# The last modulation sections between the sets of chunk inverses, and the second norm's columns inside the first half of the output projection

## The chip, the cores and the metric

One core of a Trainium2 chip runs the whole layer in one launch. The metric is device microseconds of one execution; the kernel before was timed in three runs.

## The reference

One layer of a diffusion backbone over 512 latent tokens (T) and 256 context tokens (TC), width 2048 (D), all in float32. The parts that matter here:

```python
mod = (jax.nn.silu(c) @ w_mod[l] + b_mod[l])[:, None, :]
sh1, sc1, g1, sh2, sc2, g2 = jnp.split(mod, 6, axis=-1)
h = modulate(x, norm_attn_g[l], sh1, sc1)
...
attn = mla_latent_attention(qn, rope_2d(qr, rope_q), keys_nope, keys_rope, values)
...
y, k_sum, _, _ = rwkv_bidirectional(r, k, v, wl, al, s_f, s_b, rw)
rwkv = rwkv_readout(y, r, k_sum, v, gl, gate_up[l], bonus_r_k[l], lnx_g[l], lnx_b[l])
x = x + g1 * (jnp.concatenate([attn, rwkv], axis=-1) @ w_out[l])
x = x + g2 * moe_ffn(modulate(x, norm_ffn_g[l], sh2, sc2), w_grp[l], b_grp[l], w_exp[l], b_exp[l], w1[l], w3[l], w2[l])
return rms_norm(x, final_norm_g)
```

`modulate(x, g, shift, scale)` is `rms_norm(x, g) * (1 + scale) + shift`. `moe_ffn` routes each token to one of 4 groups and to the best 2 of the 8 experts in it; 32 experts with weights of 2048 x 512, 2048 x 512 and 512 x 2048. The modulation's six parts are 2048 wide; sh1 and sc1 are needed at the start, g1 after the output projection, sh2 and sc2 for the router and the experts, g2 after the experts.

## The kernel before

Stages in the order of the trace: the first two parts of the modulation and the first norm; the input projection with its three-pass float32 products (`passes`, L174 to L176); within it, for each of 8 feature blocks f and two directions d, the small Gram matrices of chunks of 64 tokens; the inverses of their triangular blocks; the state chain over 12 chunks with the latent attention beside it; the readouts and the output projection in two halves (attention rows, then recurrent rows); the routing; 16 pairs of experts; the last norm.

**Modulation sections.** `mod_rest` (L510 to L527) makes the other four parts, s = 2, 4, 3, 5 in that order (g1, sc2, sh2, g2), each in four sections of 512 columns: 16 sections. A section is 8 loads of 512 KB issued by POOL (L519), 16 multiplications on ACT (L521), 15 additions on POOL (L523), the bias (L524, L525) and a store to `modr` in DRAM (L526). Its tiles are the five planes of `scr_`. `NM = (6, 0, 0)` lets 6 sections run before the feature blocks; the other 10 are drained after the solves are written down, so beside the chain.

**Chunk inverses.** `solve` (L459 on) inverts 32 x 32 blocks by substitution, 31 steps of a product and a sum (L479, L480), between loads of `r_ab` (L466) and stores to `r_tt` and `r_tn`; `SOLVES` has three sets. POOL makes sets 0 and 1 for both directions (one pass each) after the feature blocks 3 and 5, and set 2 for direction 0; DVE makes set 2 for direction 1. On POOL the tiles are again the planes of `scr_`; a pass ends with a copy (L483).

**Chain and filler.** `run_chain` has 12 steps for each direction. A step loads its factors on SP's queue (QXr, Lr, QYr, AYr and the inverses TNr, TFr), and multiplies: X (L813), Yp (L830), Zp (L842), Sp (L851), Yq (L865); pp and p2 (L796, L803) prepare the inverse of the next step. Yp and Yq exist from the fifth step on. Between these the generator `filler` gives pieces of attention (`mla`: sp are the scores, ptt the transposed probabilities, po the values' product) and then of the first half of the output projection (`attn_out`, `out_loop(0, ...)`: 32 units of 12 products, po_s, po_a, po_o and po_w by PSUM bank). A scheduler decides from this text, when the kernel is built, what each engine's queue holds in which order; tiles with the same buffer keep the order of the text. The last eight units use the same three PSUM banks ("rw") as the chain and the readouts.

**Readouts and second half.** `readout` (L868 to L892) treats 64 tokens: two products with `bones` (rom L882, rov L886), a square root on ACT, a reciprocal on DVE (L888) and four more DVE operations. Then `cat` is split from Y and `out_loop(1, ...)` makes the second half (po_r), with `route_chunk` after every 512 columns.

**The second norm's columns.** `cols` holds 1 + sc2 times the norm's gain, and sh2, as columns. They are made from the partial sums in `modr` by products with a column of ones (L1271, pcl, 4 products of one column for each of 8 loads `mr` on SP's queue, one buffer), written down after the output projection's first half and before its second.

Of the kernel before, what the change touches and what calls it, by code (L numbers as in the profile page):

```python
# [9 lines left out]
F32 = mybir.dt.float32  # L10
# [4 lines left out]
OP = mybir.AluOpType  # L15
# [4 lines left out]
D = 2048  # L20
# [4 lines left out]
C = 64  # L25
NT = T + TC
NP0 = 2
NM = (6, 0, 0)
NFILL = 12
NEARLY = 8  # L30
XU = 8
# [49 lines left out]
def layer(ctx, tc, tab, x, c, ctx_in, c_ctx, w_mod, b_mod, norm_attn_g, norm_ffn_g, w_in, shift_mu,  # L81
# [5 lines left out]
    ve, sc, gp, te, sy = nc.vector, nc.scalar, nc.gpsimd, nc.tensor, nc.sync  # L87
# [6 lines left out]
    modr = dram.tile([128, 4 * D], F32, name="modr")  # L94
# [30 lines left out]
    ones = cp.tile([128, 128], F32, name="ones")  # L125
# [29 lines left out]
    def bank(name, shape, tag, bufs):  # L155
        return ps[tag].tile(shape, F32, name=name, tag=tag, bufs=bufs)
# [129 lines left out]
    with tc.tile_pool(name="p0", bufs=1, side="right") as p0:  # L286
# [52 lines left out]
        n = 0  # L339
# [44 lines left out]
        for src, n, dst, g, width, a, b in ((cqT, 4, r_cq, qg, 512.0, 0, 512),):  # L384
# [5 lines left out]
            v, r, u = nv[:, 0:m], nr[:, 0:m], nu[:, 0:m]  # L390
# [35 lines left out]
        for src, n, dst, g, width, a, b in ((ckvT, 2, r_ckv, kvg, 256.0, 0, 512),  # L426
# [6 lines left out]
            v, r, u = nv[:, 0:m], nr[:, 0:m], nu[:, 0:m]  # L433
# [681 lines left out]
    def mod_row(pool, name, s, tags, e1=ve.tensor_copy):  # L1115
        t_ = pool.tile([128, D], F32, name=name)
        sc.dma_start(t_, modr[:, (s - 2) * D:(s - 1) * D])
        for n in range(4):
            pr_ = bank("prr", [128, 512], *tags[n % len(tags)])
            te.matmul(pr_, ones, t_[:, 512 * n:512 * n + 512], start=True, stop=True)  # L1120
            (sc.copy if n % 2 else e1)(t_[:, 512 * n:512 * n + 512], pr_)
        return t_
# [3 lines left out]
    late = {}  # L1126
# [4 lines left out]
    def out_loop(hf, cat, tags, after=None):  # L1131
        wo, xm = late["wo"], late["xm"]
        for n in range(4):
            ns = slice(512 * n, 512 * n + 512)
            po = tags(n)
            for k in range(8):
                raw = wo.tile([128, 512], F32, name="wor", bufs=4)
                w_ = [wo.tile([128, 512], F32R, name=f"wo{i}", bufs=3) for i in range(2)]
                sc.dma_start(raw, wo_v[:, 8 * hf + k, ns])
                split(w_[0], w_[1], raw, ve)  # L1140
                for i in range(4):
                    passes(po[i], [c_[:, k, 128 * i:128 * i + 128] for c_ in cat], w_, k == 0, k == 7)
                late["w"] = w_[1]
                yield
            for i in range(4):
                t_ = wo.tile([128, 512], F32, name="wt_", bufs=2)
                ve.tensor_mul(t_, po[i], late["g1r"][:, ns])
                ve.tensor_add(xm[:, i, ns], xm[:, i, ns], t_)
            if after:
                after(n)  # L1150
# [7 lines left out]
    def attn_out():  # L1158
        xmp = late["xmp"] = ctx.enter_context(tc.tile_pool(name="xmp", bufs=1))
        wo = late["wo"] = wos.enter_context(tc.tile_pool(name="wo", bufs=1))  # L1160
        cat = cat_tiles()
        for k in range(8):
            t_ = wo.tile([128, T], F32, name="wt_", bufs=2)
            sc.dma_start(t_, r_at[k])
            split(cat[0][:, k], cat[1][:, k], t_)
        late["ro"] = ros.enter_context(tc.tile_pool(name="ro", bufs=1))
        xm = late["xm"] = xmp.tile([128, 4, D], F32, name="xm")
        units = out_loop(0, cat, tags_a)
        xv = x[0].rearrange("(i p) d -> p i d", p=128)
        for u in range(32):  # L1170
            next(units)
            yield
            if u % 8 == (XG if u < 8 else XH):
                ns = slice(512 * (u // 8), 512 * (u // 8) + 512)
                ve.tensor_copy(xm[:, :, ns.start:ns.start + 1], late["w"][:, None, 0:1].to_broadcast([128, 4, 1]))
                for i in range(0, 4, XI):
                    sy.dma_start(xm[:, i:i + XI, ns], xv[:, i:i + XI, ns])
            if u == XG:
                late["g1r"] = mod_row(wo, "g1r", 2, [("a", 1)])
        yield from units  # L1180

    def filler():
# [66 lines left out]
    def t(name, shape, dt=F32, bufs=1):  # L1249
        return rp.tile(shape, dt, name=name, bufs=bufs)  # L1250
# [6 lines left out]
    cst = t("cst", [128, 36])  # L1257
    sy.dma_start(cst[:, 0:4], bass.AP(tensor=b_grp.tensor, offset=b_grp.offset, ap=[[0, 128], [1, 4]]))
    sy.dma_start(cst[:, 4:36], bass.AP(tensor=b_exp.tensor, offset=b_exp.offset, ap=[[0, 128], [1, 32]]))
    gc = t("gc", [128, 4, 4])  # L1260
    sy.dma_start(gc, norm_ffn_g[0].rearrange("(n p j) -> p n j", p=128, j=4))
    cols = xmp.tile([128, 2, 4, 4], F32, name="cols")
    scc, shc = cols[:, 0], cols[:, 1]
    pcl = bank("pcl", [128, 2, 4, 4], "tr", 2)
    for s in range(2):
        for n in range(4):
            mr = t("mr", [128, 512])
            sy.dma_start(mr, modr[:, (2 - s) * D + 512 * n:(2 - s) * D + 512 * n + 512])
            mv = mr.rearrange("t (p j) -> t j p", j=4)
            for j in range(4):  # L1270
                te.matmul(pcl[:, s, n, j:j + 1], mv[:, j], ones[:, 0:1], start=True, stop=True)  # L1271
    fetch(NY + NA)
    ve.tensor_copy(cols, pcl)
    ve.scalar_tensor_tensor(scc, scc, 1.0, gc, op0=OP.add, op1=OP.mult)
    wrs = t("wrs", [128, 4, 4, 36])
    ve.tensor_mul(wrs, wr, scc[:, :, :, None].to_broadcast([128, 4, 4, 36]))
    ve.tensor_mul(wr, wr, shc[:, :, :, None].to_broadcast([128, 4, 4, 36]))
# [412 lines left out]
```

## Time and profile before

| | us |
|---|---|
| median of 3 runs (lowest to highest) | 2669.04 (2664.29 to 2672.88) |
| the profiled execution | 2665.13 |
| its span | 2663.3 |
| PE busy | 2411.0 (91%) |
| DVE busy | 1406.2 (53%) |
| ACT busy | 914.1 (34%) |
| POOL busy | 737.8 (28%) |

The share of an engine over the whole span says little here, since the stages have different limits; the rows below are by stretches of the span. Times in the rows are microseconds from the span's start. The granted clock is that of PE, 1.00 being 2.4 GHz.

### The profile page before, as it was taken

The numbers are of one execution on the slowest core, as the hardware profiler recorded it, in microseconds if no ns is written. First come the engines' busy times: TensorE is split into PE (matmuls) and PEld (weight loads), VectorE is DVE, ScalarE is ACT, GpSimd is POOL, SyncE is SP. The second block draws the span as 40 slices with busy tenths as digits, with TensorE's granted clock in tenths as the row PEclk, the third lists the DMA queues.
The fourth block names the chain that finished last, engine by engine and source line by source line (L and its number), as shares of the span: only waits on it lengthen the run. The fifth ranks groups of instructions, "written<-read, shape, count | busy, mean of one in ns | idle before, by whom it ended". The sixth has DMA issues, their size and how long they took to land. (4 is left out here: it accounts for less than half of the span.)

```text
span 2663.3 us, 39444 instructions
## 1 busy us (share of the span) xinstructions
PE 2411.0 (91%) x15238; PEld 1535.9 (58%) x15238; DVE 1406.2 (53%) x2094; ACT 914.1 (34%) x1659; POOL 737.8 (28%) x830
## 2 busy tenths in 40 slices
PE   4999899998997789998968997999999999999995
PEld 2567678887876667777736785434333334334332
DVE  3345687666778767666458545243333334334324
ACT  4245564332333256554534332311111112112202
POOL 1046654016677544554535300000000000000000
PEclk9999999998997789999989997999999999999998
DMA  8965577665667768788687532999999999999995
GB/s 307 345 189 173 190 195 185 135 141 131 150 136 183 175 180 224 223 243 237 189 271 216 193 131 106 411 421 421 421 421 420 418 421 420 420 416 417 420 421 212
DMA packets 521998, 727.50 MB, mean 273 GB/s; under 512 B 320792, under 2 KB 399536, under 8 KB 471376
## 3 DMA queue, kind: packets, MB, share of 16 engines
q1 hardware_dynamic: 410512, 578.97, 62.0%
q0 software_dynamic: 24208, 83.50, 9.5%
q10 hardware_dynamic: 87088, 62.48, 8.1%
q8 instruction: 121, 1.98, 0.3%
q14 instruction: 69, 0.57, 0.1%
HBM read 659.69 MB, written 73.54 MB: 275 GB/s over the span
## 5 line engine op out<-in xcount | busy, mean ns | idle before, releaser
L523 POOL TENSOR_TENSOR scr<-scr 128x512 f32<-128x512 f32 x240 | 327.7, 1365 | 350.5 <-ACT scr L521 331.2
L174 PE MATMUL acc<-hT,w 128*128 128x512 f32 (+1 forms) x752 | 268.7, 357 | 13.0 <-DVE km L276 9.9
L175 PE MATMUL acc<-hT,w 128*128 128x512 f32 (+1 forms) x752 | 268.9, 358 | 0.0
L176 PE MATMUL acc<-hT,w 128*128 128x512 f32 (+1 forms) x752 | 268.3, 357 | 0.0
L1455 POOL DMA_INDIRECT xg<-r_x,ix x16 | 19.1, 1196 | 831.1 <-DVE sp L1440 627.3
L521 ACT ACTIVATE scr<-scr,scl 128x512 f32<-128x512 f32 x256 | 170.4, 715 | 174.8 <-DMA scr<-in_w_mod_dram 140.6
L1600 PE MATMUL py<-ew,gT 128*64 128x512 f32 x680 | 213.8, 607 | 7.9 <-ACT gT L1580 6.7
L1500 DVE TENSOR_TENSOR xm<-xm,pox 128x512 f32<-128x512 f32 x256 | 161.4, 682 | 62.1 <-PE pox L1499 61.5
L171 DVE TENSOR_TENSOR w<-wraw,w 128x512 fp32r<-128x512 f32 (+1 forms) x132 | 110.8, 845 | 140.8 <-ACT w L170 139.7
L1575 DVE SCALAR_TENSOR_TENSOR scr<-ph,ga,scr 128x512 f32<-128x512 f32 x16 | 12.0, 751 | 310.4 <-PE ph L1556 310.4
L1490 DVE TENSOR_TENSOR yt<-py,g2r 128x512 f32<-128x512 f32 x64 | 42.7, 687 | 242.1 <-PE py L1600 228.7
L174 PEld LDWEIGHTS acc<-hT,w 128*128 128x128 f32 (+1 forms) x752 | 144.5, 192 | 36.2 <-issue 15.4
L176 PEld LDWEIGHTS acc<-hT,w 128*128 128x128 f32 (+1 forms) x752 | 143.9, 191 | 22.4 <-issue 1.4
L175 PEld LDWEIGHTS acc<-hT,w 128*128 128x128 f32 (+1 forms) x752 | 144.5, 192 | 20.4 <-issue 1.0
L170 ACT CAST w<-wraw 128x512 fp32r<-128x512 f32 (+1 forms) x132 | 80.5, 613 | 217.7 <-PE acc L175 125.3
L1600 PEld LDWEIGHTS py<-ew,gT 128*64 128x64 f32 x680 | 73.5, 138 | 125.7 <-issue 109.2
L519 POOL DMA_DIRECT2D scr<-in_w_mod_dram x128 | 92.9, 726 | 173.7 <-DVE scr L358 140.7
L170 ACT CAST yr<-yt 128x512 fp32r<-128x512 f32 x64 | 39.3, 619 | 294.3 <-DVE yt L1490 293.0
L479 POOL TENSOR_TENSOR scr<-scr 128x31 f32<-128x31 f32 (+15 forms) x155 | 108.5, 700 | 27.7 <-DMA scr<-r_ab 16.0
L480 POOL TENSOR_TENSOR scr<-scr 128x31 f32<-128x31 f32 (+15 forms) x155 | 108.1, 697 | 12.1
L1498 PE MATMUL pox<-yr,ohT 128*128 128x512 f32 x256 | 105.6, 428 | 4.1 <-ACT yr L170 3.8
L1572 ACT ACTIVATE scr<-ph 128x512 f32<-128x512 f32 x16 | 9.6, 597 | 260.2 <-PE ph L1556 260.2
(702 smaller groups left out, 5381.9 us busy)
## 6 DMA issues: line engine op xcount, KB each, us to landing
ew<-in_w_dram SPq DMA_DIRECT2D x279, 1024.0 KB, 19.8
Y<-in_w_dram SPq DMA_DIRECT2D x70, 1024.0 KB, 19.5
scr<-in_w_mod_dram POOLq DMA_DIRECT2D x128, 512.0 KB, 5.3
scr<-in_w_dram SPq DMA_DIRECT2D x34, 1024.0 KB, 19.8
ld<-in_w_mod_dram SPq DMA_DIRECT2D x32, 1024.0 KB, 7.3
wraw<-in_w_in_dram ACTq DMA_DIRECT2D x104, 256.0 KB, 3.5
wor<-in_w_out_dram ACTq DMA_DIRECT2D x64, 256.0 KB, 3.3
QXr<-r_qx SPq DMA_DIRECT2D x24, 512.0 KB, 6.0
```

The source lines that it names most:

```text
L170: sc.copy(hi, src)
L171: (lo_eng or ve).tensor_sub(lo, src, hi)
L174: te.matmul(out, lhs[0], rhs[0], start=first, stop=False)
L175: te.matmul(out, lhs[0], rhs[1], start=False, stop=False)
L176: te.matmul(out, lhs[1], rhs[0], start=False, stop=last)
L479: e.tensor_mul(z, xs.to_broadcast([128, n, m]), ms.to_broadcast([128, n, m]))
L480: e.tensor_add(xo, xo, z)
L521: sc.mul(wt[:, k] if kt + k else macc, wt[:, k], scl[:, kt + k:kt + k + 1])
L523: gp.tensor_add(macc, macc, wt[:, k])
L1498: te.matmul(po, ohT[0:np_, 128 * i:128 * i + 128], yr[0], start=True, stop=False)
L1500: ve.tensor_add(xm[:, i, ns], xm[:, i, ns], po)
L1600: te.matmul(pys[n][64 * e:64 * e + 64], gT[:, j, 64 * e:64 * e + 64], ws[e][:, n], start=(j == 0), stop=(j == 3))
```

## The change

`NM` becomes `(6, 3, 3)`: three modulation sections are written down after set 0 of the inverses, three after set 1; the last four are drained after set 2, as ten were before. The columns are made by a new function inside `attn_out`, after units 10 and 18 of the first half, with loads on ACT's queue and a PSUM bank that the first half uses; their old place before the second half is gone.

```diff
-NM = (6, 0, 0)
+NM = (6, 3, 3)
...
         units = out_loop(0, cat, tags_a)
+        cols = late["cols"] = xmp.tile([128, 2, 4, 4], F32, name="cols")
+
+        def mod_cols(s):
+            if s == 0:
+                late["gc"] = wo.tile([128, 4, 4], F32, name="gc")
+                sc.dma_start(late["gc"], norm_ffn_g[0].rearrange("(n p j) -> p n j", p=128, j=4))
+            pcl = bank("pcl", [128, 4, 4], "a", 1)
+            for n in range(4):
+                mr = wo.tile([128, 512], F32, name="wt_", bufs=2)
+                sc.dma_start(mr, modr[:, (2 - s) * D + 512 * n:(2 - s) * D + 512 * n + 512])
+                mv = mr.rearrange("t (p j) -> t j p", j=4)
+                for j in range(4):
+                    te.matmul(pcl[:, n, j:j + 1], mv[:, j], ones[:, 0:1], start=True, stop=True)
+            ve.tensor_copy(cols[:, s], pcl)
+            if s == 0:
+                ve.scalar_tensor_tensor(cols[:, 0], cols[:, 0], 1.0, late["gc"], op0=OP.add, op1=OP.mult)
+
...
             if u == XG:
                 late["g1r"] = mod_row(wo, "g1r", 2, [("a", 1)])
+            if u in (10, 18):
+                mod_cols(0 if u == 10 else 1)
...
-    gc = t("gc", [128, 4, 4])
-    sy.dma_start(gc, norm_ffn_g[0].rearrange("(n p j) -> p n j", p=128, j=4))
-    cols = xmp.tile([128, 2, 4, 4], F32, name="cols")
+    cols = late["cols"]
     scc, shc = cols[:, 0], cols[:, 1]
-    pcl = bank("pcl", [128, 2, 4, 4], "tr", 2)
-    for s in range(2):
-        for n in range(4):
-            mr = t("mr", [128, 512])
-            sy.dma_start(mr, modr[:, (2 - s) * D + 512 * n:(2 - s) * D + 512 * n + 512])
-            mv = mr.rearrange("t (p j) -> t j p", j=4)
-            for j in range(4):
-                te.matmul(pcl[:, s, n, j:j + 1], mv[:, j], ones[:, 0:1], start=True, stop=True)
     fetch(NY + NA)
-    ve.tensor_copy(cols, pcl)
-    ve.scalar_tensor_tensor(scc, scc, 1.0, gc, op0=OP.add, op1=OP.mult)
```

The built order shows where POOL's work went. POOL's queue at the end of the first set of inverses, before (scr are the planes of `scr_`):

```order
L480 TENSOR_TENSOR scr<-scr 128x31
L483 COPY scr<-scr 128x1024
L467 MEMSET scr 128x1024
L468 MEMSET scr 128x32
L466 DMA scr<-r_ab 32x1024
L466 DMA scr<-r_ab 16x1024 x4
```

And the same place now, up to the second set, with the repeating middle left out:

```order
L480 TENSOR_TENSOR scr<-scr 128x31
L483 COPY scr<-scr 128x1024
L519 DMA scr<-in_w_mod_dram 128x2x512 x2
L523 TENSOR_TENSOR scr<-scr 128x512 x2
...
L524 DMA scr<-in_b_mod_dram 1x16x32
L523 TENSOR_TENSOR scr<-scr 128x512 x2
L467 MEMSET scr 128x1024
L468 MEMSET scr 128x32
L525 TENSOR_TENSOR scr<-scr 1x512
L526 DMA modr<-scr 128x512
L913 MEMSET SV_8201 64x8x64 x2
L913 MEMSET SV_8217 64x8x64 x2
```

Three sections stand between the first set's last copy and the second set's loads; three more stand in the same way between the second and the third set. The memsets of the chain's first tiles (L913) moved ahead of the second set.

PE's queue at the chain's first products, before (p is the p2 of the text, po and pqn belong to the attention):

```order
L1079 MATMUL ptt<-k_ident,p 128x128 x8
L803 MATMUL p_8320<-TFr,pps 32x32 x16
L813 MATMUL X<-SV_8201,QXr 64x64 x11
L174 MATMUL po<-pT_7582,vv_7060 128x256
L813 MATMUL X<-SV_8201,QXr 64x64 x5
L813 MATMUL X<-SV_8217,QXr 64x64 x4
```

And now (po_s is a product of the first half of the output projection, L1181 is the new place of pcl):

```order
L174 MATMUL po_s<-wo_13550,cat_12984 128x512
L803 MATMUL p_8320<-TFr,pps 32x32 x16
L813 MATMUL X<-SV_8201,QXr 64x64 x16
L813 MATMUL X<-SV_8217,QXr 64x64 x16
L1181 MATMUL pcl<-ones,wt__13481 128x1 x4
L1181 MATMUL pcl<-ones,wt__13487 128x1 x2
L842 MATMUL Zp<-Xs,TFr 64x64 x32
```

All of the attention and 14 of the 32 units of the first half moved ahead of the first X; 10 more units stand among the first four steps.

PE's queue in a late step of the chain (the ninth), before (sp is a product of the scores):

```order
L813 MATMUL X<-SV_10237,QXr 64x64 x16
L813 MATMUL X<-SV_10251,QXr 64x64 x16
L830 MATMUL Yp<-QYr,SV_10237 64x64 x7
L174 MATMUL sp<-kn_10423,qn_10326 128x512
L175 MATMUL sp<-kn_10424,qn_10326 128x512
L176 MATMUL sp<-kn_10423,qn_10327 128x512
```

And a late step now, in full:

```order
L813 MATMUL X<-SV_11145,QXr 64x64 x16
L813 MATMUL X<-SV_11159,QXr 64x64 x16
L830 MATMUL Yp<-QYr,SV_11145 64x64 x16
L842 MATMUL Zp<-Xs,TFr 64x64 x16
L830 MATMUL Yp<-QYr,SV_11159 64x64 x16
L842 MATMUL Zp<-Xs,TFr 64x64 x16
L796 MATMUL pp<-TNr,AXr 32x32 x16
L851 MATMUL Sp<-SV_11145,Lr 64x64 x16
L796 MATMUL pp<-TNr,AXr 32x32 x16
L851 MATMUL Sp<-SV_11159,Lr 64x64 x16
L803 MATMUL p_11871<-TFr,pps 32x32 x16
L865 MATMUL Yq<-AYr,SV_11145 64x64 x16
```

Only the chain's own products are left in the last eight steps. Behind the last step stand the eight readouts, and behind these the last eight units of the first half.

## Rows read from the trace of the kernel before

**Rows 1.** Busy time in stretches; x counts instructions, then PE's clock, DMA share, GB/s.

```profile
core 0: us, PE busy (x) PEld busy (x) DVE busy (x) ACT busy (x) POOL busy (x), PEclk, DMA share, GB/s
200.00:250.00 50.00, 47.10 (x246) 38.11 (x245) 22.77 (x27) 25.82 (x42) 32.19 (x29) 0.99 0.58 171
400.00:450.00 50.00, 49.27 (x268) 41.34 (x268) 39.76 (x44) 21.95 (x35) 29.59 (x27) 0.93 0.81 193
690.00:850.00 160.00, 145.10 (x779) 117.74 (x778) 129.54 (x151) 61.47 (x90) 115.29 (x158) 0.91 0.72 160
960.00:1340.00 380.00, 356.46 (x5739) 285.93 (x5738) 236.94 (x390) 210.84 (x410) 199.67 (x190) 0.96 0.77 218
1340.00:1498.00 158.00, 119.55 (x422) 84.11 (x422) 111.84 (x125) 64.62 (x106) 76.92 (x70) 0.89 0.75 237
1664.00:2646.00 982.00, 942.60 (x3924) 383.64 (x3920) 336.59 (x556) 198.62 (x435) 17.84 (x15) 1.00 0.99 408
```

**Rows 2.** POOL in order of time: start, duration, then idle time and its releaser.

```profile
706.35 1.97 POOL L483 COPY scr<-scr 128x1024 f32<-128x1024 f32 x1
...
736.22 0.49 POOL L466 DMA_DIRECT2D scr<-r_ab  x1 [19.87 <-DMA r_ax<-AX]
...
854.76 2.59 POOL L483 COPY scr<-scr 128x1024 f32<-128x1024 f32 x1
...
872.92 0.97 POOL L466 DMA_DIRECT2D scr<-r_ab  x2 [10.12 <-DMA r_ax<-AX]
...
933.28 2.02 POOL L483 COPY scr<-scr 128x1024 f32<-128x1024 f32 x1
```

**Rows 3.** The store that ends a modulation section, on POOL in order of time.

```profile
194.49 0.58 POOL L526 DMA_DIRECT2D modr<-scr  x1
...
238.59 0.57 POOL L526 DMA_DIRECT2D modr<-scr  x1
...
388.95 0.57 POOL L526 DMA_DIRECT2D modr<-scr  x1 [0.30 <-POOL scr L525]
...
444.29 0.59 POOL L526 DMA_DIRECT2D modr<-scr  x1 [0.20 <-POOL scr L468]
...
991.99 0.57 POOL L526 DMA_DIRECT2D modr<-scr  x1
...
1254.03 0.57 POOL L526 DMA_DIRECT2D modr<-scr  x1
```

**Rows 4.** PE in order of time: chain products and the first readout.

```profile
971.61 0.91 PE L813 MATMUL X<-SV,QXr 128*64 128x64 f32 x22
...
1109.28 0.69 PE L796 MATMUL pp<-TNr,AXr 32*32 32x32 f32 x32
...
1121.03 1.15 PE L813 MATMUL X<-SV,QXr 128*64 128x64 f32 x32
...
1153.54 3.52 PE L813 MATMUL X<-SV,QXr 128*64 128x64 f32 x64
...
1338.23 1.13 PE L882 MATMUL rom<-Y,k_bones 128*128 128x512 f32 x2
```

**Rows 5.** DMA from 1120 to 1250 us: SP's queue, and one kind of load.

```profile
q1 hardware_dynamic: 27874, 19.24, 54.9%
...
QXr<-r_qx SPq DMA_DIRECT2D x8, 512.0 KB, 6.6
```

**Rows 6.** DVE in order of time: reciprocals of two readouts, one between them.

```profile
1376.02 3.35 DVE L888 RECIPROCAL sq<-sq 128x512 f32<-128x512 f32 x1 [0.72 <-ACT sq L887]
...
1391.60 3.35 DVE L888 RECIPROCAL sq<-sq 128x512 f32<-128x512 f32 x1 [1.27 <-ACT sq L887]
```

**Rows 7.** PE in order of time: last eight units, then the columns' products.

```profile
1470.99 0.61 PE L174 MATMUL po_w<-wo,cat 128*128 128x512 f32 x2
...
1495.09 0.39 PE L176 MATMUL po_a<-wo,cat 128*128 128x512 f32 x1
1499.75 2.00 PE L1271 MATMUL pcl<-ones,mr 128*128 128x1 f32 x8 [4.28 <-issue]
...
1548.29 1.80 PE L1271 MATMUL pcl<-ones,mr 128*128 128x1 f32 x8
```

**Rows 8.** One group of the page's fifth part: busy, mean ns, idle before, releaser.

```profile
L521 ACT ACTIVATE scr<-scr,scl 128x512 f32<-128x512 f32 x256 | 170.4, 715 | 174.8 <-DMA scr<-in_w_mod_dram 140.6
```

## The prediction

> **What bounds the kernel now.** I read the stretches first. From 1664 us to the end the sixteen DMA engines are busy 0.99 of the time and move 408 GB/s [rows 1]: the expert weights stream in, and whatever the engines do there is hidden behind them. So a microsecond won or lost before the experts begin moves the end by one, and the question is only when the second half of the output projection can start, since it and the routing (1498 to 1664 us) follow in one piece. Before that lie three stretches. Up to about 935 us POOL makes the chunk inverses in three sets, and the last set is what the state chain waits for: its copy ends at 935.30 us (933.28 + 2.02) and the chain's first product X starts at 971.61 us [rows 2, 4]. From 960 to 1340 us the twelve steps of the chain run with the attention in their gaps, and PE is busy 356.46 of 380 us (0.94) at a granted clock of 0.96: this stretch is bound by PE's work, not by the chain's waits [rows 1]. From 1340 to 1498 us the eight readouts run beside the first half of the output projection, PE busy 119.55 of 158 us. The last matmul of that half ends at 1495.5 us [rows 7], and I use this as the mark: what the mark moves, the end moves.
>
> **Three sections before the second set.** POOL ends set 0 at 708.32 us [rows 2]. In the new order three modulation sections stand next on POOL, and all of them use the five scratch planes that the solves use, so nothing can pass them. A section took 44.1 us between two stores at 194 and 239 us, and 55.3 us between those at 389 and 444 us [rows 3]. DVE was busy 22.77 of 50 us beside the first and 39.76 of 50 beside the second; in 690 to 850 us it is busy 129.54 of 160, the same 0.8 as beside the slow one [rows 1]. So I take 54 us, with 44 and 55.3 as the ends. 708 + 3 (the stores of the set must land) + 162 = 873 us. What is queued behind: ACT does 16 multiplies a section at 715 ns, and over 16 sections it waited 140.6 us for their loads, 8.8 us a section [rows 8]. Three sections put 34 us of work and 26 us of waits among the weight casts of the input projection, where ACT is busy 61 of 160 us; I cost this at nothing, because what comes next waits for POOL anyway. If that cover were gone it would be at most the 26 us of waits.
>
> **Second set, three more sections, third set.** The second set ran from its last load at 736.22 to 857.35 us, 121 us, in two passes [rows 2]; with 3 us of loads it goes from 873 to 997 us. The 19.87 us that it waited for a store before is gone, since the store is long done. Three more sections, now beside attention: between the stores at 991.99 and 1254.03 us five sections took 52.4 us each [rows 3]; 157 + 3 gives 1157 us. The third set took 62.4 us from its last load, 65 us with loads: 1222 us. From the end of the set to the first X it took 36.3 us before; PE's queue is emptier there now, I take 30: **the chain starts at 1252 us instead of 971.6**. That is the price of the move, 280 us on POOL in front of the chain. The small memsets of the chain's first tiles were moved ahead of it and cost nothing.
>
> **What hides it.** PE doesn't stand still: the order puts the three remaining pairs of attention heads and 14 of the 32 units of the output projection ahead of the first X, and 10 more units between the first four steps. But that was the work that stood in the chain's gaps, and from the fifth step on the chain now runs alone. Its own PE work: 32 records of an X group take 1.15 us, of a pp group 0.69 us [rows 4]. A late step has 64 records each of X, Yp, Zp, Sp and Yq (5 times 2.3) and of pp and p2 (2 times 1.4): 14.3 us; a step before the fifth has no Yp and Yq, 9.7 us. Its loads: the SP queue kept the DMA engines busy 54.9% of 130 us in which 8 QXr loads were issued, that is four steps, 17.8 us a step [rows 5]. So a late step alone costs at least 17.8 us by its loads, and at most what it cost with attention between, (1338.23 - 971.61) / 12 = 30.6 us. I take 20 us, near the loads, because each load can only be issued when the product before it has freed its buffer. An early step I take at 18 us: 9.7 us, 7 us for two and a half units, and a little wait. The chain: 4 x 18 + 8 x 20 = 232 us, end at 1484 us, against 1338 before.
>
> **After the chain.** Before, readouts and projection shared the 158 us. Now the eight readouts stand alone: two gaps between reciprocals took 15.58 us together, 7.8 us each [rows 6], so 58 us to the last variance. Then the last eight units of the first half, which need the banks that chain and readouts held: 24.5 us (1470.99 to 1495.48) [rows 7]. 1484 + 58 + 24.5 = 1566 us for the mark, against 1495.5: **71 us later**.
>
> **The columns.** 32 one-column products leave the second half of the projection. They stood there as eight groups of 1.80 us [rows 7] in a stretch where PE is busy without a break: 14.4 us saved, bounds 0 (if DVE or the weight casts take over as bound) and 18.7 (with the 4.28 us of idle time before the first group, which I think is the change of PSUM pools and stays). The same products in the first half go into idle time of PE between chain steps: nothing, at most 14.4 us. Their eight loads move from the SP queue to ACT's, one load of the norm's gain with them: SP issues loads of 0.3 us less each in a stretch where it waits, nothing.
>
> **Sum.** +71 - 14.4 = +57 us on the profiled execution's 2665.1 us (span 2663.3): 2722 us. The median of the runs is 3.9 us above that execution, which is inside what I can tell.
>
> **A rule against the change.** From 1340 to 1498 us, where PE had gaps and was busy 119.55 of 158 us, the granted clock was 0.89 against 0.96 before it [rows 1], and at the lower of the two levels, 1.2 GHz, 64 X records took 3.52 us where they take 2.30 at 2.4 GHz [rows 4]. The Trainium skill, "TensorE: Matmul & The Clock Gate", section on how HAM oscillation bites in real kernels, says that a matmul loop with idle gaps between its bursts falls back to the lower clock at every gap. By that rule the chain alone would run at the lower clock from its fifth step to the end of the readouts; by the row it would keep about 0.89, and I go by the row. The rule's time is rival two.
>
> **Rivals.** One, the other side: PE stays the bound and the work is only put in another order. PE had 356 + 119 = 476 us of work from 960 us to the mark; at the 0.94 of the middle stretch that ends 507 us after 960, at 1467 us: -28 - 14.4, 2622 us. For it speaks that attention and half the projection fill the wait for POOL; against it the lonely last eight steps and the readouts, where nothing is left to fill PE with. It wins from the point where the chain ends before 1427 us (1495.5 + 14.4 - 24.5 - 58), 57 us earlier than I think: sections at 44 us give 55 of these. Two, the chain at the lower clock: PE's 14.3 us become 14.3 x 3.52 / 2.30 = 21.9, a step 24 us instead of 20 late and 22 instead of 18 early (+48 us), and the last eight units nearly twice as long (+22): 2792 us. Three, the loads: the last four sections of the modulation now run from 1222 us beside the chain, 16.8 MB, 77 us at the 218 GB/s of the chain's stretch [rows 1]. Half of that not hidden is +38 us: 2760 us. That the change doesn't reorder POOL is excluded, the order shows it.
>
> **How the numbers follow.** Forecast 0.62 (2722 us), rival one 0.08, two 0.15, three 0.15. The unknown terms of the forecast are six sections (down to -55, up to +7), twelve steps (8 late ones at 17.8 give -18, at 24 +32), the wait from set to first X, and the columns (-4, +14). The range 2672 to 2790 leaves out rival one, the upper half of rival two and a thin tail. A measurement here can tell about 0.3%, 8 us. Faster by more than that: 0.08, rival one and nothing of the forecast. Within it: 0.07, the forecast's low end. Slower: 0.85.
>
> **What would show it.** In the changed kernel: the copies that end the second and third set near 997 and 1222 us (873 if sections move for free, then I am wrong at the first step); first X near 1252 us, with PE's wait there on POOL's or the inverse's load, not on attention; X to X about 20 us in the last eight steps; the first readout near 1484 us, reciprocals 7.8 us apart; PE busy clearly below 0.8 from 1320 to 1540 us and its clock below 0.9; no one-column products in the second half, and that half about 14 us shorter. I am wrong if the first X comes before 1200 us or the chain alone takes less than 190 us.

## The result, and the profile after

The changed kernel takes 2821.66 us (median; 2816.96 to 2825.04) where the kernel before took 2670.96 us on the same chip: ratio 1.0574, 95% interval [1.0543, 1.0604]. It is slower, as forecast, but by 151 us instead of 57, and outside the range of the prediction. The profiled execution took 2825.04 us, its span 2823.2 us, 159.9 us more than before.

The mark of the prediction, the last matmul of the first half of the output projection, comes at 1669.3 us (1495.5 before, 1566 forecast). From the mark to the first `ph` product of the experts it is 146.3 us (1815.63 - 1669.3) where it was 160.3, and from there to the end 1007.6 us where it was 1007.5. So the whole loss lies ahead of the mark, +174 us, and 14 us come back behind it. The mark and the first `ph`, on PE in order of time:

```profile
1668.90 0.39 PE L176 MATMUL po_a<-wo,cat 128*128 128x512 f32 x1
...
1815.63 1.98 PE L1563 MATMUL ph<-Y,xT__15067 128*64 128x512 f32 x4 [0.20 <-ACT xT__15067 L1490]
```

The stretches that answer to those from 960 us on in [rows 1] (PE busy, PEld, DVE, ACT and POOL busy, then PE's granted clock, DMA share, GB/s):

```profile
960.00:1230.00 270.00, 219.13 (x990) 161.03 (x988) 140.31 (x241) 111.06 (x213) 171.99 (x231) 0.83 0.28 82
1230.00:1293.00 63.00, 54.00 (x322) 42.06 (x323) 27.49 (x39) 21.20 (x38) 33.37 (x45) 0.86 0.81 242
1293.00:1400.00 107.00, 93.51 (x1461) 80.01 (x1456) 60.87 (x93) 45.41 (x86) 54.45 (x50) 0.80 0.90 254
1400.00:1500.00 100.00, 59.50 (x1498) 55.57 (x1495) 34.75 (x54) 37.69 (x71) 48.58 (x46) 0.71 0.87 240
1500.00:1585.00 85.00, 71.84 (x1909) 67.00 (x1904) 43.44 (x72) 20.33 (x47) 0.00 (x0) 0.79 0.83 214
1585.00:1672.00 87.00, 49.55 (x119) 26.39 (x119) 63.97 (x66) 19.09 (x30) 1.09 (x5) 0.74 0.45 128
sum 712.00, PE 547.52 PEld 432.05 DVE 370.83 ACT 254.78 POOL 309.48; mean PE 91.25 PEld 72.01 DVE 61.80 ACT 42.46 POOL 51.58
```

From 960 us to just behind the mark, before had 538 us with PE busy 476.0 and idle 62.0 [rows 1]; after has 712 us with PE busy 547.5 and idle 164.5. The 174 us are thus 102 us of new idle time and 72 us of longer busy time. The work on PE is nearly the same, with some 15 us of the columns in it; it ran at a granted clock of 0.71 to 0.86, where [rows 1] has 0.96 and 0.89. The first line is attention without the chain (PE busy 0.81, DMA share 0.28: of PE's 51 idle us 22.1 are waits for its own softmax, p on ACT); lines three to five are the chain without attention (DMA share 0.83 to 0.90), in the first of them with ten units of the projection.

POOL's queue in order of time, the ends of sections (L526) and of passes of the inverses (L483), answering to [rows 2, 3]:

```profile
715.21 1.97 POOL L483 COPY scr<-scr 128x1024 f32<-128x1024 f32 x1
788.93 0.57 POOL L526 DMA_DIRECT2D modr<-scr  x1
846.71 0.57 POOL L526 DMA_DIRECT2D modr<-scr  x1
931.70 0.59 POOL L526 DMA_DIRECT2D modr<-scr  x1 [0.30 <-POOL scr L525]
...
1052.33 1.96 POOL L483 COPY scr<-scr 128x1024 f32<-128x1024 f32 x1
...
1203.63 0.59 POOL L526 DMA_DIRECT2D modr<-scr  x1 [0.20 <-POOL scr L468]
1253.24 2.11 POOL L483 COPY scr<-scr 128x1024 f32<-128x1024 f32 x1
```

The first three sections took 214 us (717.2 to 931.7), the second set 123, the next three sections 149, the third set 52. The longest wait of that first stretch (waiter, what it waited for, total, times, longest):

```profile
POOL scr L523 <- ACT scr L521: 105.3, 14, 16.2
```

POOL waited for ACT's multiplications half of the time. ACT's own queue in the third section shows why (ACTq are loads that ACT's queue issues):

```profile
874.05 1.33 ACT L521 ACTIVATE scr<-scr,scl 128x512 f32<-128x512 f32 x2
...
883.40 0.48 ACTq L1004 DMA_DIRECT2D wraw<-in_w_ukv_dram  x1
883.92 0.62 ACT L170 CAST cqn<-p 128x512 fp32r<-128x512 f32 x1 [8.55 <-DVE AY L651]
887.87 1.50 ACT L669 COPY L<-pq 128x1024 f32<-128x1024 f32 x2 [3.33 <-PE pq L668]
889.25 0.63 ACT L170 CAST cqn<-p 128x512 fp32r<-128x512 f32 x1
891.97 0.58 ACT L1015 COPY p<-pqr 128x512 f32<-128x512 f32 x1 [2.08 <-PE pqr L176]
892.65 0.58 ACT L679 COPY rs<-pb 128x512 f32<-128x512 f32 x1
895.70 0.72 ACT L684 ACTIVATE rs<-rs,pc 128x512 f32<-128x512 f32 x1 [2.46 <-DVE rs L683]
896.33 1.32 ACT L521 ACTIVATE scr<-scr,scl 128x512 f32<-128x512 f32 x2
```

Between two pairs of multiplications of 0.7 us lie 21 us, in which ACT did 5 us of other work and waited for DVE and PE 16 us (8.55, 3.33, 2.08 and 2.46). A queue keeps its order, so POOL got its next block only then.

PE where the chain starts, then some of its twelve steps and the first readout, answering to [rows 4]:

```profile
1275.30 0.24 PE L796 MATMUL pp<-TNr,AXr 32*32 32x32 f32 x2 [0.23 <-DMA TNr<-r_tn]
...
1292.99 2.08 PE L813 MATMUL X<-SV,QXr 128*64 128x64 f32 x64
...
1400.07 2.19 PE L813 MATMUL X<-SV,QXr 128*64 128x64 f32 x36
1428.46 1.76 PE L813 MATMUL X<-SV,QXr 128*64 128x64 f32 x33
1465.57 1.65 PE L813 MATMUL X<-SV,QXr 128*64 128x64 f32 x26
1495.11 2.08 PE L813 MATMUL X<-SV,QXr 128*64 128x64 f32 x64
1515.42 1.79 PE L813 MATMUL X<-SV,QXr 128*64 128x64 f32 x54
...
1584.75 2.07 PE L882 MATMUL rom<-Y,k_bones 128*128 128x512 f32 x2
```

The first X comes at 1293.0 us (971.6 before), the chain takes 291.8 us (366.6 before, with attention in it). Its first four steps take 107 us, the next three 28, 37 and 30, the last five 20.3 and less. PE reached the chain's first products at 1275 us and waited only 0.23 us for the inverses: POOL and PE's own queue were ready at the same time.

### The profile page after: what moved, and what is told of

Its sections match the earlier page's. It is cut to its first block, busy times and chain, and to the rows that moved or that the text cites. A ratio compares the mean times of both kernels' runs of the same rounds, so it can differ in the third digit from the quotient of the medians.

```text
span 2823.2 us, 39528 instructions
## 1 busy us (share of the span) xinstructions
PE 2477.2 (88%) x15238; PEld 1592.5 (56%) x15238; DVE 1413.7 (50%) x2095; ACT 913.8 (32%) x1659; POOL 720.4 (26%) x830
## 5 line engine op out<-in xcount | busy, mean ns | idle before, releaser
L523 POOL TENSOR_TENSOR scr<-scr 128x512 f32<-128x512 f32 x240 | 333.5, 1389 | 364.0 <-ACT scr L521 347.4
L174 PE MATMUL acc<-hT,w 128*128 128x512 f32 (+1 forms) x752 | 273.7, 364 | 12.6 <-DVE km L276 9.7
L175 PE MATMUL acc<-hT,w 128*128 128x512 f32 (+1 forms) x752 | 273.5, 364 | 0.0
L176 PE MATMUL acc<-hT,w 128*128 128x512 f32 (+1 forms) x752 | 272.2, 362 | 0.1
L174 PEld LDWEIGHTS acc<-hT,w 128*128 128x128 f32 (+1 forms) x752 | 147.7, 196 | 37.2 <-issue 15.1
L176 PEld LDWEIGHTS acc<-hT,w 128*128 128x128 f32 (+1 forms) x752 | 146.9, 195 | 23.8 <-issue 2.1
L175 PEld LDWEIGHTS acc<-hT,w 128*128 128x128 f32 (+1 forms) x752 | 147.6, 196 | 21.1 <-issue 1.2
L480 POOL TENSOR_TENSOR scr<-scr 128x31 f32<-128x31 f32 (+15 forms) x155 | 101.0, 651 | 12.2
L479 POOL TENSOR_TENSOR scr<-scr 128x31 f32<-128x31 f32 (+15 forms) x155 | 94.2, 608 | 28.6 <-DMA scr<-r_ab 16.9
L171 DVE TENSOR_TENSOR wo<-wor,wo 128x512 fp32r<-128x512 f32 x64 | 50.0, 787 | 99.8 <-ACT wo L170 93.2
```

The lines of the kernel that those rows point to most:

```text
L171: (lo_eng or ve).tensor_sub(lo, src, hi)
L174: te.matmul(out, lhs[0], rhs[0], start=first, stop=False)
L175: te.matmul(out, lhs[0], rhs[1], start=False, stop=False)
L176: te.matmul(out, lhs[1], rhs[0], start=False, stop=last)
L479: e.tensor_mul(z, xs.to_broadcast([128, n, m]), ms.to_broadcast([128, n, m]))
L480: e.tensor_add(xo, xo, z)
```

## The experiments

Theory one: the six sections delay the third set on POOL, and what is lost is the overlap of chain and attention. Theory two: the sections cost in their new places, by ACT's queue and their loads. Theory three: the chain alone is slowed by the last four sections' loads beside it. All times below are medians, "more" is against the kernel before in the same comparison.

**The two parts apart.** First the columns alone:

```diff
-NM = (6, 3, 3)
+NM = (6, 0, 0)
```

> The columns inside the first half, but all ten sections again behind the solves (NM back to 6, 0, 0). If the price is the delay of the third set by the six sections and the columns are a gain of their own, the eight groups of 1.80 us leave the second half and cost nothing in the gaps of the chain: 14 us less than before, about 2656 us. If the columns' products cost in the chain's busy stretch what they saved later, it is the time before, 2668 to 2673 us. If the columns have a part in the changed kernel's long early steps, it is slower than before, up to 2690 us.

Measured: 2667.84 us, ratio 1.0011 [0.9986, 1.0037]. No gain. In the profiled execution, the longest of the twelve (2676.93 us), the mark comes 25 us later than before (1520.8) and the second half is 13 us shorter. The products stand here behind the last readout, eight groups on PE from 1444 to 1489 us.

In that stretch PE is not idle. From the last readout's products to the mark (before, then columns alone):

```profile
1429.00:1498.00 69.00, 61.68 (x256) 48.43 (x254) 49.78 (x59) 30.75 (x51) 43.74 (x37) 0.98 0.68 214
```

```profile
1427.00:1523.00 96.00, 86.49 (x338) 71.44 (x336) 61.28 (x69) 32.94 (x55) 51.11 (x44) 0.89 0.63 204
```

The eight groups went from one busy stretch of PE to another. Then the sections alone, `NM = (6, 3, 3)` in the kernel before:

> The kernel before with NM = (6, 3, 3), the columns in their old place. If the sections carry the whole price, the mark (last matmul of the first half) is 174 us later as in the changed kernel and the second half keeps its 14 us: 2836 to 2846 us. If the columns between the first chain steps made part of the price, it is below the changed kernel's 2822 us, with the first four steps shorter than their 107 us.

Measured: 2819.16 us, 1.0572 [1.0529, 1.0615], below the expected 2836 and the same as the changed kernel's 1.0574. The sections carry the whole price, and the columns are worth nothing beside them that could be told (the two intervals are 8 and 11 us to each side): without them the chain's first four steps take 91.5 us (1271.9 to 1363.4) instead of 107.1, with them the second half is 14 us shorter. A trace of one execution has its limits here: the first set ends 10.8 us earlier in this profile than in the changed kernel's, though both programs are the same up to there.

**What slows a section between the sets.** The six moved sections multiply on POOL instead of ACT (here and in the next such cut the condition that picks these six is left out):

```diff
-sc.mul(wt[:, k] if kt + k else macc, wt[:, k], scl[:, kt + k:kt + k + 1])
+gp.tensor_scalar_mul(wt[:, k], wt[:, k], scl[:, kt + k:kt + k + 1])
 gp.tensor_add(macc, macc, wt[:, k])
```

> The changed kernel, but the six moved sections are multiplied on POOL (a multiplication in place and an addition, both 128 x 512) and no longer on ACT. If ACT's queue set the pace of the sections (72, 58 and 85 us for the first three, where POOL waited 105 us for ACT), a section now takes two POOL operations of about 1.2 us for each of 16 blocks, 35 to 42 us, the second set ends 60 to 90 us earlier, the first X comes 80 to 130 us before 1293 us and the time falls by 60 to 110 us, to 2710 to 2760 us. If the loads set the pace, the sections stay at 50 us or more and the time is above 2790 us. If only the chain beside the last four sections is at fault, the time falls by less than 20 us.

Measured: 2879.93 us, 1.0805 [1.0755, 1.0854], slower than the changed kernel; the sections took 78, 76 and 112 us. It doesn't tell the theories apart, since two new costs came with it. From 715 to 930 us, POOL's groups (busy, mean ns, idle before):

```profile
L527 POOL TENSOR_SCALAR scr<-scr,scl 128x512 f32<-128x512 f32 x36 | 68.4, 1906 | 23.7 <-DMA scr<-in_w_mod_dram 23.7
L528 POOL TENSOR_TENSOR scr<-scr 128x512 f32<-128x512 f32 x33 | 50.2, 1522 | 1.3
...
L920 POOL MEMSET SV<- 64x512 f32 x4 | 2.1, 518 | 42.0 <-DVE Y L479 41.8
```

A multiplication and an addition take 3.4 us on POOL, not 2.4, and the memsets of the chain's first tiles, which the new order put into the third section, waited 41.8 us for memory that DVE's solve still used. So the next kernel leaves the multiplications of the six sections out, and puts those memsets on DVE:

```diff
-sc.mul(wt[:, k] if kt + k else macc, wt[:, k], scl[:, kt + k:kt + k + 1])
 gp.tensor_add(macc, macc, wt[:, k])
...
-gp.memset(st_[0, d]["SV"][half_[hh], :, hh, :], 0.0)
+ve.memset(st_[0, d]["SV"][half_[hh], :, hh, :], 0.0)
```

> The changed kernel, but the six moved sections do no multiplication on ACT (POOL adds the loaded blocks as they are; the scaling is left out), and the memsets of the chain's first tiles stand on DVE. If POOL waits in a section for ACT's queue (105 of the 215 us of the first three), a section is left with 16 operations of 1.4 us and 8 issues of 0.7 us, 30 to 40 us: the third set ends at about 1110 us for 1255, and the time falls to 2690 to 2740 us. If the loads set the pace, sections stay at 50 us or more and the time is above 2790 us.

Measured: 2796.10 us, 1.0488 [1.0453, 1.0522], and neither expectation holds whole: the time is above 2790 us, but not because the sections kept their length. The first three sections took 150 us instead of 214, the next three 117 instead of 149: 64 us of the first three went with the multiplications, and the loads and POOL's own work set a floor of 38 to 60 us a section. But the third set ended only 40 us earlier, at 1215.6, because the second set took 182 us instead of 123: its first pass's stores on SP's queue came late. POOL, in order of time:

```profile
928.27 1.98 POOL L483 COPY scr<-scr 128x1024 f32<-128x1024 f32 x1
986.58 0.95 POOL L467 MEMSET scr<- 128x1024 f32 x1 [56.33 <-DMA r_tt<-scr]
...
1004.66 1.92 POOL L466 DMA_DIRECT2D scr<-r_ab  x4 [15.52 <-DMA r_tn<-scr]
```

SP's queue keeps its order, and in front of these stores it waited for DVE's own solve and for an attention output's store:

```profile
SPq L486 <- DMA r_at<-ao: 16.8, 1, 16.8
SPq L485 <- DVE Y L480: 15.2, 1, 15.2
```

And of the 40 us only 12 arrived at the first X (1280.7), which PE's queue now reached 65 us after the set: attention and 14 units of the projection stand ahead of it. So the sections on POOL are not the only thing that sets the start; the order on PE that was built with them is a second one, as late.

**Loads beside the chain.** The last four sections do one of their eight loads:

```diff
-for kt in range(0, KT, 2):
+for kt in range(0, KT if s < 5 else 2, 2):
```

> The changed kernel, but the last four sections (g2) load and add only the first of their eight blocks; seven eighths of that sum are left out. In the changed kernel these four run from 1256 to 1485 us, beside the chain, and the steps beside them take 28, 37 and 30 us where the steps after them take 20, 20, 19 and 17. If their 16.8 MB slow the chain, the late steps all take 17 to 21 us, the chain is 40 to 70 us shorter than its 292 us and the time falls to 2750 to 2785 us. If the chain's pace is its own (its loads, its waits, the clock), the steps stay and the time is above 2810 us.

Measured: 2775.81 us, 1.0415 [1.0367, 1.0464], 46 us less than the changed kernel. The first X is where it was (1290.4), the first four steps take 92 us for 107, the last eight 156 for 185. From 1400 to 1500 us, the DMA queues (packets, MB, share; q1 is the chain's loads, q0 the sections') and the busy times, first of the changed kernel, then of this one:

```profile
q1 hardware_dynamic: 24017, 15.49, 59.9%
q0 software_dynamic: 2208, 8.26, 25.9%
```

```profile
1400.00:1500.00 100.00, 80.96 (x2184) 75.30 (x2184) 51.23 (x87) 25.93 (x60) 0.00 (x0) 0.81 0.86 222
...
q1 hardware_dynamic: 32500, 21.87, 84.2%
```

The DMA engines are equally busy, 0.87 and 0.86; what the sections took, 26%, the chain takes when they are gone, and PE is busy 81 us instead of 59.5. The last four sections thus cost the chain 44 us. But the edit takes their multiplications on ACT away together with their loads, and the waits of the changed kernel say how they cost. First three waits from 1293 to 1585 us, then ACT and PE (last line) around one of them:

```profile
ACT scr L521 <- DMA scr<-in_w_mod_dram: 82.3, 23, 11.1
PE Yp L830 <- ACT Xs L815: 17.4, 2, 9.0
PE Sp L851 <- DMA Lr<-r_l: 0.6, 1, 0.6
```

```profile
1439.52 1.33 ACT L521 ACTIVATE scr<-scr,scl 128x512 f32<-128x512 f32 x2 [11.12 <-DMA scr<-in_w_mod_dram]
1440.87 0.58 ACT L815 COPY Xs<-X 128x512 f32<-128x512 f32 x1
1441.51 1.97 PE L830 MATMUL Yp<-QYr,SV 128*64 128x64 f32 x32 [8.40 <-ACT Xs L815]
```

The chain's copy of X stands on ACT behind two multiplications of a section, these wait for the section's load, and PE waits for the copy. Each of PE's seven waits for ACT between 1400 and 1500 us, 32 us together, ends with a copy that stands right behind such a multiplication. From 1293 to 1585 us PE waited 40 us for ACT's copies and 1.2 us for the chain's own loads. Without seven eighths of the sections' work it is 4 and 13 us in the 249 us from 1290 on. So theory three holds for 44 us in its size, but the way there is mainly ACT's queue, of which theory two spoke, and not a chain whose own loads come late. A kernel with the loads beside the chain and without the multiplications was not tried.

**Delay alone.** The kernel before with all sections where they were, but the zeros in the chain's first tiles made from the last attention output:

```diff
-gp.memset(st_[0, d]["SV"][half_[hh], :, hh, :], 0.0)
+ve.tensor_scalar_mul(st_[0, d]["SV"][half_[hh], :, hh, :],
+                     late["aol"][half_[hh]].rearrange("p (f v) -> p f v", f=NF), 0.0)
...
+    while "ro" not in late:
+        next(fill)
```

The last two lines write all of the attention down ahead of the chain.

> The kernel before with all its sections in their old places (NM = 6, 0, 0, columns late), but the zeros of the chain's first tiles are made as 0 times the last attention output, so that the chain can't start before attention is done. No set of inverses is later. If the price of the change is that attention and chain no longer run in each other's gaps, attention alone ends at about 1210 us, the chain starts 20 us later, and the time is 2780 to 2830 us, as the changed kernel's. If the price comes from the sections in their new places (ACT's queue, the loads, POOL), it is far below: under 2730 us.

Measured: 2757.71 us, 1.0328 [1.0291, 1.0364], between the two expectations. No set is late here (the third ends at 942.0 us), and the first X comes at 1216.1 us. The stretches up to X, and the chain:

```profile
942.00:1190.00 248.00, 209.38 (x1050) 153.50 (x1050) 128.49 (x234) 131.07 (x248) 146.03 (x141) 0.84 0.42 127
...
1216.00:1482.00 266.00, 207.21 (x3812) 173.52 (x3814) 146.23 (x215) 110.04 (x208) 115.75 (x107) 0.85 0.91 263
```

Attention alone keeps PE busy 0.84 at a clock of 0.84, much as in the changed kernel's first line. So 91 of the 151 us come without any section in a new place, from a chain that starts 245 us later; the other 60, by difference, come with a start 77 us later still. Four sections run beside the chain here too (the last store at 1464.8 us), so what they cost it is in the 91.

**Is there a free part?** Three sections in one place only, then one, and four more ahead of the feature blocks:

> The changed kernel with NM = (6, 0, 3): three sections between the second and the third set, none between the first and the second. The third set then ends about 150 us later than before (1085 us for 935) and the chain starts at about 1115 us, while attention still has work for its gaps. If a delay of the chain costs in proportion (151 us for 321 us of later first X in the changed kernel), it is 70 us: 2735 to 2750 us. If a delay is free as long as attention is left to fill the gaps, it is 2665 to 2695 us.

> The changed kernel with NM = (6, 3, 0): three sections between the first and the second set only. They took 215 us in the changed kernel, so the third set ends about 200 us later than before, at 1120 to 1140 us, and the chain starts at about 1160 us. In proportion this is 90 us: 2750 to 2770 us. If a delay is free as long as attention is left, 2670 to 2710 us. If the sections ahead of the second set also hold the input projection's end (their multiplications in ACT's queue), it is dearer than the place after it by more than the later start says, above 2770 us.

> The changed kernel with NM = (6, 1, 0): one section between the first and the second set. The third set ends about 55 to 65 us later than before, at about 995 us, the first X at about 1030 us. Three sections in one place gave 66 and 70 us more than the time before for a first X 164 and 149 us later, six gave 151 for 321: 0.40 to 0.47 us for each us. If every microsecond costs like that, one section costs 25 us: about 2692 us. If there is a free part at the start, because attention and the chain together have slack to take it, one section costs under 8 us: 2660 to 2675 us.

> The kernel before with NM = (10, 0, 0), columns in their old place: four sections more ahead of the feature blocks, where POOL stood idle 140 us, and six instead of ten beside the chain. Two more cost nothing (0.9985). Four take about 220 us, 80 more than the idle time, so the first set's loads come at about 665 us instead of 590. If the later start of the chain is what counts, the second and third set take up 20 to 30 us of it in their waits, the first X comes 40 to 60 us later and the time is 15 to 27 us longer: 2682 to 2695 us. If fewer sections beside the chain are worth more than that, it is under 2667 us.

| NM, columns | third set ends | first X later by | us more | ratio, interval |
|---|---|---|---|---|
| 6,1,0, early | 970.0 | 30.3 | 13.8 | 1.0046 [1.0030, 1.0063] |
| 10,0,0, late | 983.3 | 54.2 | 11.1 | 1.0059 [1.0039, 1.0080] |
| 6,0,3, early | 1092.2 | 149.0 | 70.5 | 1.0290 [1.0235, 1.0344] |
| 6,3,0, early | 1094.5 | 163.5 | 66.1 | 1.0270 [1.0224, 1.0316] |
| 6,0,0, late, chain behind attention | 942.0 | 244.5 | 91.2 | 1.0328 [1.0291, 1.0364] |
| 6,3,3, late | 1239.1 | 300.3 | 155.9 | 1.0572 [1.0529, 1.0615] |
| 6,3,3, early | 1255.4 | 321.4 | 150.7 | 1.0574 [1.0543, 1.0604] |

Where sections stand between the sets, each microsecond by which the chain starts later costs 0.40 to 0.52 us on average. A free part of 30 us is excluded: one section costs 8 to 17 us by its interval. One of a few us can't be told, as the first X of the four kernels with six or eight sections in front and none between the sets lies between 962 and 972 us. The front place with ten sections costs 0.20 by the medians and 0.29 by the ratio; that it costs less because six instead of ten sections are left to load beside the chain was not tried. The place between the first and second set is not dearer than the one behind it: theory two, as far as it speaks of the input projection's end, falls. One section cost 14 us for an expected 25, since the third set came 35 us later and not 55 to 65; three ahead of the second set cost 66 for an expected 90, since it came 159 us later and not 200.

**Where a section is free.** Two more sections ahead of the feature blocks, with early and with late columns:

```diff
-NM = (6, 3, 3)
+NM = (8, 0, 0)
```

> The changed kernel with NM = (8, 0, 0): the columns early, two more sections ahead of the feature blocks, none between the sets. In the kernel before POOL stands idle there, from the last early section to the first load of the first set, 140 us. If a moved section costs only where POOL is on the path to the chain, these two cost nothing and the time is that of the columns alone, about 2656 us, or a few us less, since eight instead of ten sections load beside the chain. If a section costs wherever it stands (16 multiplications of 715 ns and their waits in ACT's queue, 4 MB of loads), it is 10 to 40 us slower than the columns alone.

> The kernel before with NM = (8, 0, 0), the columns in their old place. With early columns the same gave 0.9983 [0.9959, 1.0007] of the time before, and early columns alone 1.0011 [0.9986, 1.0037]. If the two sections ahead of the feature blocks shorten the chain's stretch a little and the columns do nothing either way, it is 2656 to 2664 us. If early columns hide a gain or a loss of their own, it differs from the time with early columns by over 6 us, one way or the other.

Measured: 2661.86 us, 0.9983 [0.9959, 1.0007], and 2663.57 us, 0.9985 [0.9965, 1.0005]. The sections end at 496.6 and 550.8 us, and POOL still waits for the first set's last block (from 444 to 600 us, then the same in the kernel before):

```profile
POOL scr L466 <- DMA r_ab<-AX: 34.7, 1, 34.7
```

```profile
POOL scr L466 <- DMA r_ax<-AX: 70.1, 2, 67.2
POOL scr L466 <- DMA r_ab<-AX: 66.8, 1, 66.8
```

They cost nothing, and they gain nothing that these comparisons could tell from no change; a version that beats both kernels was not found.

## Why the prediction was right, and where it was wrong

**Right.** The sign and its reason: what the mark moves, the end moves, and the chain, made to start late, is left with nothing in its gaps. From the chain's end to the mark it took 84.5 us (1584.75 to 1669.3), forecast 82.5, with the reciprocals 8.3 us apart for 7.8. The second set took 123 us for 124. The second half did become 14 us shorter, as worked out from [rows 7]. From 1320 to 1540 us PE was busy 0.74 of the time at a clock of 0.74, where it was said that they would fall below 0.8 and 0.9.

**The first wrong term, sections one to three: 165 us forecast, 214 measured.** The prediction took 54 us a section from a stretch with the same share of DVE [rows 1, 3], and costed ACT's part "at nothing". The pace was not DVE's: 64 of the 214 us went with ACT's multiplications in the experiment without them. The page of the kernel before showed this wait, in the group of POOL's additions (331.2 us in 16 sections, 21 us a section):

```profile
L523 POOL TENSOR_TENSOR scr<-scr 128x512 f32<-128x512 f32 x240 | 327.7, 1365 | 350.5 <-ACT scr L521 331.2
```

The prediction read only ACT's own group [rows 8], for what the sections do to ACT, and not what ACT's other work does to a section. The later POOL terms gave 24 us back (sections four to six 149 us for 160, third set 52 for 65), and the first set was 9 us late in this execution. Together the third set came at 1255 us for 1222.

**The second, the chain: 232 us forecast, 292 measured.** The extra cost that rival three spoke of came beside the forecast, not instead of it. Eight late steps of 20 us each are what the chain does without the sections' loads (156 us measured for 160); with them it took 185, and its first steps 15 us more. The prediction knew that the last sections run from the end of the third set, and priced their bytes in a rival with a chance of 0.15, when nothing in its own times kept them from the chain's stretch. That is 44 of the 60 us. The way was another one than bytes: PE waited 40 us for the chain's copies on ACT, most of them right behind a section's multiplications, the same handover as in the first term. The lower bound of 17.8 us a step by loads was not one either: the eleventh step took 17.2 us (1554.57 to 1571.73). The rest lies mainly in the first four steps: 92 us without the sections' loads, for 72 forecast. PE is busy there 93.5 of 107 us at a clock of 0.80, so they are mostly bound by PE's work, to which ten units and the columns belong; in the kernel without columns there they are 15.6 us shorter. How the remainder splits between clock and waits was not tried.

**The third, the columns: -14.4 forecast, no gain that could be measured.** What the second half won the first half lost, in the changed kernel in the chain's early steps, with columns alone behind the readouts. That they "go into idle time of PE" was wrong: PE is busy 0.87 and 0.90 of the time in these two stretches. The bound that the prediction kept, at most 14.4 us for the new place, is close to the 15.6 us by which the early steps differ with and without them.

**A right number for half a reason.** From the third set to the first X it took 37.6 us for 30 forecast. The prediction let POOL alone set the start; PE's queue was as late, 0.23 us apart, so a faster POOL would not have helped by much, as the kernel without multiplications showed (40 us earlier on POOL, 12 at X). And its way of costing, a late chain less the attention that no longer stands in it, hid the simple size: 0.40 to 0.52 us for each us of delay. That fits the shares of PE's time, 0.81 for attention alone and 0.60 to 0.85 for the chain's last eight steps alone, where both together filled 0.94 [rows 1].

Rival two, the lower clock, holds in part: from 1400 to 1500 us the granted clock is 0.71, between the two levels of 1.2 and 2.4 GHz, with PE busy 0.60; without the last sections' loads and multiplications it is 0.81 with PE busy 0.81. The Trainium skill, "TensorE: Matmul & The Clock Gate", section "HAM oscillation — how this bites in real kernels", says that gaps between bursts bring the lower clock back; the trace agrees in direction, but the mean over these 100 us stayed well above 0.50. What the clock cost was not separated from the waits.

## What to carry to other kernels

Two stages that each leave an engine waiting are worth most beside each other, and work put ahead of one of them on a side engine pulls them apart; here about half of each microsecond of delay was lost, and 30 us of it were not free either. Cost a step that passes between two engines by the in-order queue of both, with what stands between its instructions there, not by the busy share of either. Work that leaves a busy stretch of an engine has gained nothing until the rows of its new place show idle time, and work whose start is moved must be costed in the stretch where it lands, by every queue that it stands in there and not by its bytes alone.

## What the hardware did that was not expected

- A 128 x 512 multiplication by a column took POOL 1.91 us and the addition behind it 1.52 us on average in the experiment with both on POOL; in the changed kernel the additions average 1.48 us from 717 to 932 us and 1.39 us over all 240.
- With the one-column products in it, the stretch from the last readout to the mark had a granted clock of 0.89 (columns alone), without them 0.98 (before). Beside 64 products of one column the stretch holds 18 more of the projection (270 for 252); that the products of one column are the cause was not tried.
- A store of POOL's results, issued through SP's queue behind another engine's stores, landed so late that POOL stood still 56 and 15 us in the kernel without multiplications.
